# Two transformer blocks on one core: the branch for overfull experts moves behind the expert pass, and four handovers between stages are ordered anew

## The chip, the core and the metric

The kernel runs on one core of a Trainium2 chip. The core has a matrix engine (TensorE, in the profile PE, its weight loads PEld), three other compute engines (VectorE or DVE, ScalarE or ACT, GpSimd or POOL) and a queue engine (SyncE or SP) that issues most of the transfers from memory. Each engine takes its own instructions in order; semaphores tie them together. The metric is the device time of one execution in microseconds (us), as the median of several runs.

## The reference

The input is one sequence of 256 tokens of width 1024, in fp32. Two blocks follow each other.

The first block has two layers. Each layer is a mixer (four kinds of attention, each on a quarter of the width) and a feed-forward part, both behind an RMS norm whose gain, shift and output gate come from a conditioning vector:

```python
x = x + g_m * (concat(o_a, o_b, o_c, o_d) @ w_out[l])
hn = adaln(x, ffn_norm_g[l], sh_f, sc_f)
f = swiglu(hn, ...) if l % 2 == 0 else moe_swiglu(hn, router, w1, w3, w2)
x = x + g_f * f
```

The feed-forward part of layer 0 is dense (width 2816). That of layer 1 is a mixture of 8 experts (width 3584): a router picks two experts for each token, and the output is the sum of their SwiGLU outputs, weighted by the softmax of the two logits. The first block ends in an RMS norm.

The second block is a dense FFN, an attention mixer (8 heads of neighbourhood attention, 8 heads of dilated attention, 64 wide) and another dense FFN, each with a norm before and after it:

```python
h = swiglu_2(rmsnorm_2(x, pre_g), w_gate, w_up, w_down)
x = x + 0.5 * rmsnorm_2(h, post_g)
```

## The kernel before, in words

The 256 tokens are two tiles of 128 (`t` = 0 and 1), held as `x[t]` with tokens on the partitions. A matrix product needs its left side with the width on the partitions, so each stage first transposes `x[t]` on PE and writes `hT[t]`.

**Products in three passes.** To keep fp32 accuracy, each operand is split into a rounded part `hi` and a rest `lo`, and `mm3` (lines 213 to 217) does three matmuls: hi by hi, hi by lo, lo by hi. Weights come in granules of at most 1 MB, 128 partitions by 2048 columns (`wload`, line 143, on SP's queue, into `st` or `sx` tiles). `wsplit` (line 173) makes `hi` on ACT (line 181) and `lo` on DVE (line 185), in pieces of at most `wide["step"]` columns, into a few rotating pairs of tiles. In the mixers of the first block that step is 1024 columns, elsewhere 2048. So every weight passes through SP, ACT, DVE and PE, in this order.

**Order.** A scheduler orders the instructions of each engine ahead of time, by the order of the program text and a model of their durations; so weights of a later stage can be loaded and split before an earlier stage is done, as far as tiles are free. `behind(ins, first)` (line 208) forces one instruction behind another in this order, without a wait. After a norm of tile 0 (`norm_ev`, line 284, or `scaled_hT`, line 303), `hold` notes its last two instructions on ACT and DVE; the weight pieces from column 2048 to column 5120, counted from there, are put behind them (lines 186 to 192). Tile 1 has no such rule. A run-time `tc.If` is one unit for the scheduler: nothing from outside is put inside.

**Expert pass.** Each expert takes its tokens into 128 slots. `moe()` (line 1325) routes, gathers the rows of expert 0, loads a register on every engine with the largest number of tokens that any expert has (line 1414), and branches (line 1415): if it is over 128, a second pass with other slot numbers (`moe_pass` with `rnd` = 1) adds what the first 128 slots leave out. Behind this stands the common pass (`rnd` = 0): 8 experts by 7 blocks of 512 columns. For each block PE does up and gate products into two PSUM banks (`eh`), then the down products of the block before (`down`, line 1135, into two banks `eo`, one per half of the width). The outputs of experts 0 to 6 are written to DRAM and gathered back by token; they are added to `x` by `moe_combine` (line 1080), for tile 0 and tile 1 at blocks 5 and 6 of the last expert. Those of expert 7 are put back by `scatter` (line 1104) after its last product: for each half, split, two matmuls per token tile with a 0/1 matrix (`ohT`), two DVE sums per tile into `x`.

**Behind the pass.** Lines 1649 to 1658 transpose and scale `x[t]` whole, sum its squares, take the reciprocal roots, and multiply `x`; `dense_ffn` (line 454) then runs with weights g1, g3, g2. In its block 0 (256 columns) it does tile 0's gate and value products over the whole depth of 1024, then tile 1's.

**Mixer of the second block.** `mix2` (line 1440) projects q, k and v, and for each of four groups of heads transposes q into `qT` and k into a block-diagonal `kb`, zeroed by POOL before: two heads lie on partitions 0 to 63 and 64 to 127, each with 256 columns of its own, so that one matmul of 128 rows by 512 columns (line 1478) gives the logits of two heads:

```python
p = aps("lg2")
nc.tensor.matmul(p.rearrange("p (a b) -> p a b", a=2), qT[:, hp, t * T:(t + 1) * T],
                 kb[:, hp, :, :], start=True, stop=True)
```

Of the kernel before, what the change touches and what calls it, by code (L numbers as in the profile page):

```python
# [11 lines left out]
I32 = mybir.dt.int32  # L12
# [29 lines left out]
HELD_FROM = 2048  # L42
HELD = 3072
# [52 lines left out]
def kernel(ctx: ExitStack, tc: tile.TileContext, a: dict, out: bass.AP):  # L96
# [76 lines left out]
    def wsplit(ld, pool=None, pre="", late=False, after=None, into=None, at=0):  # L173
# [3 lines left out]
        step = max(n for n in (1, 2, 4) if n * w <= wide["step"])  # L177
        for k in range(0, nk, step):
# [27 lines left out]
    hold = {"ops": None, "skip": 0}  # L206
# [77 lines left out]
    def norm_ev(t, y, ps, hT, gain, shift=None):  # L284
# [15 lines left out]
        if t == 0:  # L300
            hold.update(ops=ops, skip=HELD_FROM)

    def scaled_hT(t, hT, gain):
# [10 lines left out]
        if t == 0:  # L314
            hold.update(ops=ops, skip=HELD_FROM)
# [138 lines left out]
    def dense_ffn(hT, w1, w3, w2, post, hook=None, r=None):  # L454
        with ExitStack() as es:
# [5 lines left out]
            acc = [[aps(f"fo{t}{n}") for n in range(2)] for t in range(2)]  # L461
# [13 lines left out]
            for b in range(nb + 1):  # L475
                gT = [None, None]
                if b < nb:
# [22 lines left out]
                    if b == 0:  # L500
# [69 lines left out]
    def transpose_p(ap, pt, lg, idx, nk):  # L570
        nkc = nk // T
        per_bank = 4 // nkc
        for i0 in range(0, len(idx), per_bank):
            sub = idx[i0:i0 + per_bank]
            p = hps("ptr")
            for j, i in enumerate(sub):
                for kc in range(nkc):
# [3 lines left out]
                 p[:, :len(sub) * nk].rearrange("p (a b c) -> p a b c", a=len(sub), b=nkc))  # L581

# [402 lines left out]
    def moe_turn(mp, rnd, ps, oh, tp=None, xg=None):  # L985
# [6 lines left out]
        def step(i):  # L992
# [20 lines left out]
            ohT = (tp or mp).tile([T, 256], F32R, tag="ohT", name="ohT", bufs=2)  # L1013
# [12 lines left out]
    def moe_slots(pool, posm, yd):  # L1026
        sel, gate = rt["sel"], rt["gate"]
        zero = small([T, 9], I32, name="zslot", bufs=1)
        nc.vector.memset(zero, 0)
        tab = dram.tile([T * 9, 1], I32, name="slots")  # L1030
# [4 lines left out]
        for t in range(2):  # L1035
            ok = small([T, 8], name="pok")
            nc.vector.scalar_tensor_tensor(ok, posm[t], 128.0, sel[t], op0=ALU.is_le, op1=ALU.mult)
            v = small([T, 8], name="pv")
            nc.vector.scalar_tensor_tensor(v, posm[t], 8.0, erow, op0=ALU.mult, op1=ALU.add)
            nc.vector.tensor_tensor(v, v, ok, op=ALU.mult)  # L1040
# [9 lines left out]
            none = small([T, 2], name="pnone")  # L1050
            nc.vector.tensor_scalar(none, ab, 0.0, 1025.0, op0=ALU.is_equal, op1=ALU.mult)
            put = small([T, 2], I32, name="pput")
            nc.vector.scalar_tensor_tensor(put, ab, -1.0, none, op0=ALU.add, op1=ALU.add)
            for i in range(2):
                nc.gpsimd.indirect_dma_start(tab[:, :], bass.IndirectOffsetOnAxis(ap=put[:, i:i + 1], axis=0),
                                             tok[:, t:t + 1], None)
            nc.vector.tensor_tensor(ok, ok, enot, op=ALU.mult)
# [40 lines left out]
    def moe_pass(mp, gp, rnd, gate, posm, yh, yl, grow, ld_fn, split_fn, first=None, yd=None):  # L1098
# [43 lines left out]

        nxt = first or gather(0)
        prev = None
        done = None
        for e in range(NE):
            xh, xl, ohT = nxt
            acc = [aps(f"eo{n}") for n in range(2)]
            for b in range(nb):
# [7 lines left out]
                for wi, nm in enumerate(("e1", "e3")):  # L1157
# [9 lines left out]
                    if wi == 0:  # L1167
                        nc.scalar.activation(s, p, AF.Silu)
                    else:
                        nc.vector.tensor_tensor(g, s, p, op=ALU.mult)  # L1170
                if prev is not None:
                    down(prev[1], prev[2], prev[3], gT)
                if done is not None and b == 1:
                    if rnd:
                        scatter(*done)
                    else:
                        keep(done[0], done[1])
                    done = None
                if b == 0 and e > 0:
                    done = (e - 1, prev[1], prev[4])  # L1180
# [9 lines left out]
                if b == nb - 3 and e + 1 < NE:  # L1190
# [4 lines left out]
                    turn = moe_turn(gp, rnd, None, oh, None, xg)  # L1195
# [4 lines left out]
                if e == NE - 1 and b >= 5:  # L1200
# [124 lines left out]
    def moe():  # L1325
        sel, gate = rt["sel"], rt["gate"]
        with tc.tile_pool(name="mo", bufs=1, reuse_waits="tile") as mo, \
# [34 lines left out]
            with tc.manual_schedule():  # L1362
# [37 lines left out]
                nc.vector.tensor_copy(mxi, mx)  # L1400
                trn = moe_turn(mo, 0, gp, oh)
# [12 lines left out]
            most = nc.values_load(mxi[0:1, 0:1], min_val=0, max_val=256)  # L1414
            with tc.If(most > T):  # L1415
                with tc.tile_pool(name="mq", bufs=1) as mq:
                    moe_pass(mq, mo, 1, gate, posm, yh, yl, grow,
# [377 lines left out]
```

## Time and profile before

| | us |
|---|---|
| median of 3 runs | 2085.16 (2085.03 to 2085.52) |
| profiled execution | 2086.3 |
| its span, first to last instruction | 2084.5 |
| PE busy in the span | 2015.6 |
| DVE busy | 1590.2 |
| ACT busy | 1251.4 |

The mean granted clock of PE is 0.983 of full speed. In rows of time order, an `x4` behind a row means four instructions of a kind in a row, and the bracket gives the engine's idle time before it and what ended it. A matmul's own duration is longer than the distance to the next, because matmuls overlap; the distance between two starts is what it costs. The engine names with a q (PEq, ACTq) are the engines' sequencers.

### The profile page before, as it was taken

The numbers are of one execution on the slowest core, as the hardware profiler recorded it, in microseconds if no ns is written. First come the engines' busy times: TensorE is split into PE (matmuls) and PEld (weight loads), VectorE is DVE, ScalarE is ACT, GpSimd is POOL, SyncE is SP. The second block draws the span as 40 slices with busy tenths as digits, with TensorE's granted clock in tenths as the row PEclk, the third lists the DMA queues.
The fourth block names the chain that finished last, engine by engine and source line by source line (L and its number), as shares of the span: only waits on it lengthen the run. The fifth ranks groups of instructions, "written<-read, shape, count | busy, mean of one in ns | idle before, by whom it ended". The sixth has DMA issues, their size and how long they took to land.

```text
span 2084.5 us, 24737 instructions
## 1 busy us (share of the span) xinstructions
PE 2015.6 (97%) x9369; PEld 1623.0 (78%) x9370; DVE 1590.2 (76%) x2044; ACT 1251.4 (60%) x1469; POOL 37.1 (2%) x37
## 2 busy tenths in 40 slices
PE   7999999999899999999999999999989999998998
PEld 3867888777678888888888888888768886777886
DVE  6897878797688888888888888888895446556544
ACT  3766434476377777777777777777654345655442
POOL 0000000000000000000000000001000000000000
PEclk9999999999899999999999999999999999999999
DMA  8846876484499999999999999999966534436530
GB/s 331 292 177 256 353 292 242 173 233 150 154 340 379 366 369 374 385 380 382 379 386 379 378 378 378 383 363 399 396 243 240 185 101 163 165 135 228 202 122 20
DMA packets 89809, 586.38 MB, mean 281 GB/s; under 512 B 12880, under 2 KB 13776, under 8 KB 23376
## 3 DMA queue, kind: packets, MB, share of 16 engines
q1 hardware_dynamic: 81184, 566.05, 72.2%
q10 hardware_dynamic: 6432, 11.84, 1.6%
q0 software_dynamic: 2064, 6.83, 0.9%
q8 instruction: 75, 1.23, 0.2%
q14 instruction: 54, 0.44, 0.1%
HBM read 578.89 MB, written 5.78 MB: 280 GB/s over the span
## 4 chain that ended last, share of the span: by engine, by line
PE 67%; DVE 3%; ACT 1%; issue 1%; DVEq 0%; ACTq 0%
PE eh L215 10%; PE eh L216 10%; PE eh L214 10%; PE eo L215 5%; PE eo L216 5%; PE eo L214 5%; PE ff L214 4%; PE ff L215 4%; PE ff L216 4%; PE fo L214 2%; PE fo L215 2%; PE fo L216 2%; DVE lo L185 1%; PE egt L1129 1%; PE pj L216 1%
## 5 line engine op out<-in xcount | busy, mean ns | idle before, releaser
L185 DVE TENSOR_TENSOR lo<-st,hi 128x2048 fp32r<-128x2048 f32 (+2 forms) x327 | 648.1, 2002 | 138.2 <-ACT hi L181 131.2
L181 ACT CAST hi<-st 128x2048 fp32r<-128x2048 f32 (+2 forms) x328 | 540.2, 1681 | 156.9 <-PE ff L216 58.7
L185 DVE TENSOR_TENSOR lo<-sx,hi 128x2048 fp32r<-128x2048 f32 (+1 forms) x200 | 451.8, 2274 | 131.5 <-ACT hi L181 128.8
L181 ACT CAST hi<-sx 128x2048 fp32r<-128x2048 f32 (+1 forms) x200 | 374.5, 1899 | 136.5 <-PE ff L216 97.0
L214 PE MATMUL eh<-hi,xeh 128*128 128x512 f32 x896 | 351.4, 392 | 8.2 <-PEq L1415 5.1
L215 PE MATMUL eh<-lo,xeh 128*128 128x512 f32 x896 | 353.3, 394 | 2.4 <-DVE lo L185 2.4
L216 PE MATMUL eh<-hi,xel 128*128 128x512 f32 x896 | 350.4, 391 | 0.0
L214 PE MATMUL ff<-hi,hTh 128*128 128x512 f32 (+1 forms) x576 | 221.6, 385 | 10.5 <-DVE hTl L312 4.6
L215 PE MATMUL ff<-lo,hTh 128*128 128x512 f32 (+1 forms) x576 | 217.1, 377 | 1.5 <-DVE lo L185 1.5
L216 PE MATMUL ff<-hi,hTl 128*128 128x512 f32 (+1 forms) x576 | 217.4, 378 | 0.1
L214 PEld LDWEIGHTS eh<-hi,xeh 128*128 128x128 f32 x896 | 169.1, 189 | 45.2 <-ACTq L1415 5.5
L215 PEld LDWEIGHTS eh<-lo,xeh 128*128 128x128 f32 x896 | 169.2, 189 | 41.3 <-DVE lo L185 7.1
L216 PEld LDWEIGHTS eh<-hi,xel 128*128 128x128 f32 x896 | 169.2, 189 | 34.5
L215 PE MATMUL eo<-lo,egh 128*128 128x512 f32 x448 | 179.7, 401 | 0.3 <-DVE lo L185 0.3
L214 PE MATMUL eo<-hi,egh 128*128 128x512 f32 x448 | 175.2, 391 | 0.7 <-ACT egh L220 0.7
L216 PE MATMUL eo<-hi,egl 128*128 128x512 f32 x448 | 174.9, 390 | 0.5 <-DVE egl L220 0.5
L214 PEld LDWEIGHTS ff<-hi,hTh 128*128 128x128 f32 x576 | 111.5, 194 | 29.9 <-DVE hTl L312 4.8
L214 PE MATMUL pj<-hi,hTh 128*128 128x512 f32 (+3 forms) x320 | 123.9, 388 | 4.2 <-ACT hTh L220 3.1
L215 PEld LDWEIGHTS ff<-lo,hTh 128*128 128x128 f32 x576 | 111.5, 194 | 20.0 <-DVE lo L185 2.0
L216 PEld LDWEIGHTS ff<-hi,hTl 128*128 128x128 f32 x576 | 111.2, 193 | 20.1 <-DVE hTl L220 0.4
L216 PE MATMUL pj<-hi,hTl 128*128 128x512 f32 (+3 forms) x320 | 122.7, 384 | 3.4 <-DVE hTl L220 1.9
L215 PE MATMUL pj<-lo,hTh 128*128 128x512 f32 (+3 forms) x320 | 125.1, 391 | 0.9 <-DVE lo L185 0.8
(383 smaller groups left out, 2611.3 us busy)
## 6 DMA issues: line engine op xcount, KB each, us to landing
st<-in_e_dram SPq DMA_DIRECT2D x192, 1024.0 KB, 7.4
sx<-in_e_dram SPq DMA_DIRECT2D x144, 1024.0 KB, 7.6
st<-in_ada_dram SPq DMA_DIRECT2D x30, 1024.0 KB, 5.1
sx<-in_g_dram SPq DMA_DIRECT2D x19, 1024.0 KB, 6.0
sx<-in_h_dram SPq DMA_DIRECT2D x19, 1024.0 KB, 4.9
sx<-in_ada_dram SPq DMA_DIRECT2D x18, 1024.0 KB, 10.3
st<-in_w_in_dram SPq DMA_DIRECT2D x16, 1024.0 KB, 5.0
sx<-in_f_dram SPq DMA_DIRECT2D x15, 1024.0 KB, 7.0
```

Source lines behind the costliest of these rows:

```text
L181: c = nc.scalar.copy(hi[:, d], st[:, s])
L185: d = nc.vector.tensor_tensor(*rest.pop(), op=ALU.subtract)
L214: m = nc.tensor.matmul(ps, xh, wh, start=start, stop=False)
L215: nc.tensor.matmul(ps, xh, wl, start=False, stop=False)
L216: nc.tensor.matmul(ps, xl, wh, start=False, stop=stop)
L1129: nc.tensor.transpose(p[:, j * T:(j + 1) * T], g[:, j * T:(j + 1) * T], ident)
```

## The change

1. **The branch.** The `tc.If` with the second pass stands behind the common pass. Its register loads come in the middle of that pass, at the first block of expert 6. For this, expert 7's `ohT` gets a tile that lives on, and the slot table covers 16 times 128 entries, so tokens beyond the 128 slots have a place in it (three small DVE operations fewer).
2. **The end of the pass.** For the last expert, `finish_last` does the last two blocks' down products half by half: both for half 0, then half 1, with the scatter of half 0 (`back(0)`) in between. The scatter of half 1 is returned as `rest` and called later. The two combines come at blocks 4 and 5.
3. **The start of the next FFN.** `dense_ffn` takes a function `start`. Its block 0 then runs over half the depth for both tiles and both weights, into four PSUM banks, then over the other half. `start(0)` transposes and scales half 0 of both tiles, calls `rest()`, and sums squares; `start(1)` does half 1; `start(2)` takes the roots. The norm's two sums come from `x` and from `x` times its gain, for both tiles at once.
4. **Holds.** Weight pieces from column 2048 to 5120 are put behind tile 0's last instructions, and those from 4096 to 8192 behind tile 1's. Pieces are at most 1024 columns up to column 4096 after tile 0's norm, and throughout `mix2`.
5. **Logits of the second block.** k is kept as it is, one copy per tile and no zeroing; each head's logits are a matmul of 64 rows by 256 columns, the two heads of a pair into two banks.

```diff
-HELD_FROM = 2048
-HELD = 3072
+HELD = ((2048, 5120), (4096, 8192))
+FINE = 4096
@@ wsplit
-        step = max(n for n in (1, 2, 4) if n * w <= wide["step"])
+        step = max(n for n in (1, 2, 4) if n * w <= (1024 if hold["n"] < FINE else wide["step"]))
...
-            if hold["ops"] is not None:
-                if hold["skip"] <= 0:
-                    behind(c, hold["ops"][0])
-                    behind(d, hold["ops"][1])
-                hold["skip"] -= min(step, nk) * w
-                if hold["skip"] < -HELD:
-                    hold["ops"] = None
+            for first, last, ops in hold["ops"]:
+                if first <= hold["n"] < last:
+                    behind(c, ops[0])
+                    behind(d, ops[1])
+            hold["n"] += min(step, nk) * w
@@ norm_ev, scaled_hT
-        if t == 0:
-            hold.update(ops=ops, skip=HELD_FROM)
+        holds(t, ops)
@@ dense_ffn
+                    if b == 0 and start is not None:
+                        lds = {(wi, kg): wload("f1", flat, kg) for kg in range(2) for wi, flat in enumerate((w1, w3))}
+                        p = {(t, wi): aps(f"ff{wi}{t}") for t in range(2) for wi in range(2)}
+                        for kg in range(2):
+                            start(kg)
+                            hl = pair()
+                            ws = [wsplit(lds[wi, kg], into=hl, at=wi * 4 * w) for wi in range(2)]
+                            for t in range(2):
+                                for wi in range(2):
+                                    up(p[t, wi], t, kg, ws[wi])
+                        start(2)
...
@@ moe_pass
+        def finish_last(acc, ohT, gT, g):
...
+            def back(n):
+                sl = slice(n * 512, n * 512 + 512)
+                e = wk.tile([T, D], F32R, tag="y", name="eys", bufs=2)
+                split_to(halves(e)[0], halves(e)[1], acc[n])
+                for t in range(2):
+                    p = (pps if n else hps)("sct")
+                    for i in range(2):
+                        nc.tensor.matmul(p, ohT[:, t * T:(t + 1) * T], halves(e)[i], start=i == 0, stop=i == 1)
+                    nc.vector.scalar_tensor_tensor(p, p, gate[t][:, NE - 1:NE], grow[:, sl], op0=ALU.mult, op1=ALU.mult)
+                    nc.vector.tensor_tensor(x[t][:, sl], p, x[t][:, sl], op=ALU.add)
+
+            products(0, nb - 2, gT)
+            g = transposes(g)
+            products(0, nb - 1, g)
+            products(1, nb - 2, gT)
+            back(0)
+            products(1, nb - 1, g)
+            return lambda: back(1)
...
+                if rnd == 0 and e == NE - 1 and b == nb - 1:
+                    return finish_last(acc, ohT, gT, g)
...
+                if e == NE - 2 and b == 0:
+                    rt["most"] = nc.values_load(rt["mxi"][0:1, 0:1], min_val=0, max_val=256)
...
-                if e == NE - 1 and b >= 5:
+                if e == NE - 1 and b >= 4:
                     behind(add.pop(0)(), m)
@@ moe
-            most = nc.values_load(mxi[0:1, 0:1], min_val=0, max_val=256)
-            with tc.If(most > T):
-                ...
             with tc.tile_pool(name="mp", bufs=2, reuse_waits="tile") as mp:
...
+            with tc.If(rt["most"] > T):
+                with tc.tile_pool(name="mq", bufs=1) as mq:
+                    moe_pass(mq, mo, 1, gate, posm, yh, yl, grow,
...
+        return rest
@@ mix2
-            widen(ap, MIX_PAIRS[1])
+            widen(ap, MIX_PAIRS[1], 1024)
...
+                for k in range(4):
+                    hp, i = divmod(k, 2)
+                    r = slice(i * 64, (i + 1) * 64)
+                    nc.tensor.matmul(p[i][:, hp * nk:(hp + 1) * nk], qT[r, hp, t * T:(t + 1) * T],
+                                     kT[r, hp, :nk], start=True, stop=True)
...
-                kb = ap.tile([T, 2, 2, 256], F32, tag="k2", name="k2", bufs=2)
-                nc.gpsimd.memset(kb, 0.0)
+                kb = ap.tile([T, 2, 256], F32, tag="k2", name="k2", bufs=2)
...
@@ behind the pass
+    def start1(h):
+        if h < 2:
+            for t in range(2):
+                scaled_half(t, h, hT, fgain)
+            if h == 0:
+                rest()
...
```

## Rows read from the trace of the kernel before

**Rows 1.** The page: busy time; groups with busy time, mean ns, idle before.

```profile
PE 2015.6 (97%) x9369; PEld 1623.0 (78%) x9370; DVE 1590.2 (76%) x2044; ACT 1251.4 (60%) x1469; POOL 37.1 (2%) x37
...
L185 DVE TENSOR_TENSOR lo<-sx,hi 128x2048 fp32r<-128x2048 f32 (+1 forms) x200 | 451.8, 2274 | 131.5 <-ACT hi L181 128.8
...
L181 ACT CAST hi<-sx 128x2048 fp32r<-128x2048 f32 (+1 forms) x200 | 374.5, 1899 | 136.5 <-PE ff L216 97.0
```

**Rows 2.** Stretches: length, busy times by engine, PE clock, DMA share, GB/s.

```profile
564.00:583.00 19.00, 10.59 (x27) 7.16 (x26) 10.80 (x22) 10.61 (x8) 5.17 (x5) 0.62 0.32 99
1500.00:1520.00 20.00, 17.57 (x77) 13.71 (x76) 19.09 (x13) 11.68 (x9) 0.00 (x0) 1.00 0.77 269
1520.00:1563.00 43.00, 34.11 (x177) 27.95 (x176) 39.42 (x80) 24.23 (x46) 0.00 (x0) 0.88 0.68 255
1737.00:1757.00 20.00, 15.81 (x63) 11.15 (x61) 17.30 (x50) 15.61 (x30) 0.00 (x0) 0.91 0.62 223
1760.00:1870.00 110.00, 109.10 (x560) 84.57 (x559) 57.87 (x141) 65.80 (x145) 1.90 (x2) 1.00 0.43 147
1880.00:1900.00 20.00, 14.27 (x86) 12.86 (x86) 16.23 (x48) 14.80 (x31) 0.00 (x0) 0.83 0.63 247
```

**Rows 3.** Line 1415, the branch: ns min/median/max, first and last start.

```profile
L1415 PEldq COMPARE_BRANCH  x1: 5872/5872/5872, 563.3 to 563.3; - x1
L1415 ACTq COMPARE_BRANCH  x1: 50/50/50, 564.9 to 564.9; - x1
L1415 DVEq COMPARE_BRANCH  x1: 72/72/72, 565.1 to 565.1; - x1
L1415 DVEq EVENT_SEMAPHORE  x1: 21/21/21, 568.9 to 568.9; - x1
```

**Rows 4.** PE in order of time at the start of the expert pass.

```profile
563.64 0.64 PE L1012 MATMUL ohT<-gen,oh 128*128 128x128 f32 x2
...
569.37 0.76 PE L214 MATMUL eh<-hi,xeh 128*128 128x512 f32 x1 [5.10 <-PEq L1415]
...
574.20 0.63 PE L216 MATMUL eh<-hi,xel 128*128 128x512 f32 x1
...
576.63 0.49 PE L214 MATMUL eh<-hi,xeh 128*128 128x512 f32 x1 [1.80 <-ACT hi L181]
...
582.26 0.40 PE L216 MATMUL eh<-hi,xel 128*128 128x512 f32 x1
```

**Rows 5.** PE in order of time at the end of the expert pass.

```profile
1519.85 0.39 PE L214 MATMUL eo<-hi,egh 128*128 128x512 f32 x1
...
1522.57 0.39 PE L214 MATMUL eo<-hi,egh 128*128 128x512 f32 x1
...
1541.16 1.97 PE L307 MATMUL trx<-gen,x 128*128 128x128 f32 x8 [1.68 <-DVE x L1116]
...
1542.78 0.56 PE L214 MATMUL ff<-hi,hTh 128*128 128x256 f32 x1
...
1562.31 0.40 PE L215 MATMUL ff<-lo,hTh 128*128 128x512 f32 x1
```

**Rows 6.** DVE in order of time, the scatter's sums of one half.

```profile
1535.01 1.42 DVE L1114 SCALAR_TENSOR_TENSOR sct<-sct,gate,row 128x512 f32<-128x512 f32 x2 [0.59 <-PE sct L1113]
...
1536.33 1.28 DVE L1116 TENSOR_TENSOR x<-sct,x 128x512 f32<-128x512 f32 x2
```

**Rows 7.** The page: DMA issues, KB each, median us from issue to landing.

```profile
sx<-in_g_dram SPq DMA_DIRECT2D x19, 1024.0 KB, 6.0
```

**Rows 8.** PE in order of time, logits of the second block's attention.

```profile
1771.06 3.67 PE L1478 MATMUL lg<-k,q 128*128 128x512 f32 x8 [0.32 <-ACT k L566]
```

**Rows 9.** DVE in order of time, into the last FFN.

```profile
1887.49 2.29 DVE L185 TENSOR_TENSOR lo<-sx,hi 128x2048 fp32r<-128x2048 f32 x1
```

**Rows 10.** PE in order of time: into the projections, into the last FFN.

```profile
1751.61 0.50 PE L216 MATMUL pj<-hi,hTl 128*128 128x512 f32 x1 [1.59 <-DVE hTl L312]
...
1893.59 0.58 PE L214 MATMUL ff<-hi,hTh 128*128 128x256 f32 x1 [4.60 <-DVE hTl L312]
```

More of the change, by code (lines that the diff above doesn't have):

```diff
@@ L204, in wsplit, with holds @@
         return finish
-    hold = {"ops": None, "skip": 0}
+    hold = {"ops": [], "n": 0}
+    def holds(t, ops):
+        if t == 0:
+            hold.update(ops=[], n=0)
+        hold["ops"].append((*HELD[t], ops))
     def behind(ins, first):
@@ L299, in norm_ev, with scaled_half @@
             ops = split_to(hT[t][0][:, c:c + 4, :], hT[t][1][:, c:c + 4, :], full)
-        if t == 0:
-            hold.update(ops=ops, skip=HELD_FROM)
+        holds(t, ops)
+    def scaled_half(t, h, hT, gain):
+        p = hps("trx")
+        for j in range(4):
+            nc.tensor.transpose(p[:, j * T:(j + 1) * T], halves(x[t])[h][:, j * T:(j + 1) * T], ident)
+        for j in range(4):
+            c, src = 4 * h + j, p[:, j * T:(j + 1) * T]
+            g = gain[:, c:c + 1]
+            nc.scalar.activation(hT[t][0][:, c, :], src, AF.Copy, scale=g)
+            nc.vector.scalar_tensor_tensor(hT[t][1][:, c, :], src, g, hT[t][0][:, c, :].bitcast(F32),
+                                           op0=ALU.mult, op1=ALU.subtract)
     def scaled_hT(t, hT, gain):
@@ L460, in dense_ffn @@
             es.callback(stages, None)
-            acc = [[aps(f"fo{t}{n}") for n in range(2)] for t in range(2)]
+            if start is None:
+                acc = [[aps(f"fo{t}{n}") for n in range(2)] for t in range(2)]
             nb = len(FF_BLOCKS)
@@ L581, in transpose_p, with row_logits, f @@
                  p[:, :len(sub) * nk].rearrange("p (a b c) -> p a b c", a=len(sub), b=nkc))
+    def row_logits(bank, t, nk, qT, kT):
+        p = []
+        def f(h):
+            if not p:
+                p.extend(bank(f"lgr{i}") for i in range(2))
+                for k in range(4):
[3 more added lines that the diff above has]
+                                     kT[r, hp, :nk], start=True, stop=True)
+            hp, i = divmod(h, 2)
+            return p[i][:, hp * nk:(hp + 1) * nk]
+        return f
     def pv(po, pt, heads, v, nk):
@@ L1012, in step @@
                 nc.tensor.transpose(q[:, t * T:(t + 1) * T], oh[t].bitcast(F32), ident)
-            ohT = (tp or mp).tile([T, 256], F32R, tag="ohT", name="ohT", bufs=2)
+            ohT = sml.tile([T, 256], F32R, name="ohL") if keep else (tp or mp).tile([T, 256], F32R, tag="ohT", name="ohT",
+                                                                                    bufs=2)
             nc.scalar.copy(ohT, q[:, :256])
@@ L1141, in down, with products @@
                         b == 0 and k == 0, b == nb - 1 and k == 3)
+        def finish_last(acc, ohT, gT, g):
+            def products(n, b, g):
+                ws = split_fn(ld_fn("e2", "e2", 2 * b + n, NE - 1))
+                for k in range(4):
+                    mm3(acc[n], g[0][:, k * T:(k + 1) * T], g[1][:, k * T:(k + 1) * T], *ws[k],
+                        False, b == nb - 1 and k == 3)
+            def back(n):
[15 more added lines that the diff above has]
+            return lambda: back(1)
         nxt = first or gather(0)
@@ L1147, in moe_pass @@
             xh, xl, ohT = nxt
-            acc = [aps(f"eo{n}") for n in range(2)]
+            if not rnd or e == 0:
+                acc = [aps(f"eo{n}") for n in range(2)]
             for b in range(nb):
@@ L1173, in moe_pass @@
                 if done is not None and b == 1:
[L1174 to L1177, printed above, removed]
+                    keep(*done)
                     done = None
                 if b == 0 and e > 0:
-                    done = (e - 1, prev[1], prev[4])
+                    if rnd:
+                        scatter(e - 1, prev[1], prev[4])
+                    else:
+                        done = (e - 1, prev[1])
                 prev = (g, acc, e, b, ohT)
@@ L1542, in mix2 @@
                     nc.scalar.activation(qT[:, :, t * T:(t + 1) * T], p4[:, 0:2, :], AF.Copy, scale=0.125)
-                    for g in range(2):
-                        evac(kb[g * 64:(g + 1) * 64, :, g, t * T:(t + 1) * T], p4[g * 64:(g + 1) * 64, 2:4, :])
+                    evac(kb[:, :, t * T:(t + 1) * T], p4[:, 2:4, :])
                 for t in range(2):
```

87 lines of the change are left out of this document (47 added, 40 removed).

## The prediction

> **What bounds the kernel now.** The page's busy line comes first: TensorE (PE) is at work 97% of the span, so a saving counts only where PE is seen idle, or slow, or doing work that can go [rows 1]. The stretch table says where that is: in the expert pass and in the down and up projections PE is full, and the losses sit in four short places, where one stage hands over to the next. From 564 to 583 us PE works 10.59 of 19 us at a mean granted clock of 0.62; from 1520 to 1563 us 34.11 of 43 at 0.88; from 1737 to 1757 us 15.81 of 20 at 0.91; from 1880 to 1900 us 14.27 of 20 at 0.83. The attention of the second block, 1760 to 1870 us, is full: 109.10 of 110 [rows 2]. The lines of the branch, L1415 [rows 3], and PE's order of time [rows 4, 5] then say who ends each wait. One full-rate matmul of 512 columns takes (1522.57 - 1519.85)/12 = 0.227 us, at half clock (574.20 - 569.37)/11 = 0.44 us; the 256-column ones I take at half of that.
>
> **The branch leaves the start of the pass (A).** PE ends the last transposes at 564.28 (563.64 + 0.64) and starts the first expert matmul at 569.37, after 5.10 us for PEq L1415 [rows 4]. PE's compare-and-branch takes 5872 ns where ACT's takes 50, and DVE, whose branch is at 565.1, signals only at 568.9, 3.8 us later [rows 3]. PE then does 12 matmuls at half clock, waits 1.80 us more for the next hi part, and is at full rate from 582.26, when 21 matmuls are done [rows 4]. Without the branch PE goes on at 564.3. The next hi and lo, 1.90 and 2.27 us [rows 1], can be there at 564.9 + 4.2 = 569.1, counted from where ACT's branch stood [rows 3]; at half clock the first 12 matmuls last to 569.5, so this hides them. Twelve at 0.44, nine at 0.227 and 1 us for a wait give 564.3 + 5.3 + 2.0 + 1.0 = 572.6 where 582.26 stood: 9.7 us. I take 9, for the slot work of DVE that now competes with the lo parts. Bounds: 5.1 (the wait alone) and 13 (21 at full rate). The five register loads move into the pass, where PE has matmuls queued: nothing.
>
> **The end of the pass (B).** From the first matmul of the last down products, 1519.85, to the first 512-column matmul of the next FFN, 1562.31, are 42.5 us [rows 5]. The work in them at full rate is 48 down matmuls (10.9), 8 scatter matmuls (1.8), 96 of 256 columns (10.9) and some 20 transposes (2.2, by the 256-column price): 25.8 us. So 16.7 us are waits and half clock: the scatter of both halves stands behind the last product, DVE does 1.42 + 1.28 us of it per half [rows 6], and only then come the transposes, 1.68 us late [rows 5]. After: the first half is scattered while PE does the second half's products, the second while PE does the FFN's first half. What is added is the branch. It stands behind the last 12 products, which PE holds for 2.7 us, so of its 5.87 us 3.2 show [rows 3]; DVE's 3.8 run beside that. Then 1.6 us from the transposes to the first matmul (1541.16 to 1542.78 [rows 5]), 2.6 us for half clock (the 0.88 over 43 us [rows 2]), 0.7 for the last block's turn, 1.7 for weight parts that were cut ahead of time and now may stand behind the branch; and the second combine comes one block earlier, where the first left PE 2.43 us idle (20 - 17.57 [rows 2]). Sum 25.8 + 3.2 + 1.6 + 2.6 + 0.7 + 1.7 + 2.4 = 38.0: a gain of 4.5 us. Upper bound, branch covered and combine absorbed: 25.8 + 1.6 + 2.4, a gain of 12.7. Lower bound: all 5.87 show, and a weight load (6.0 us to landing [rows 7]) and one hi and lo (1.90, 2.27 [rows 1]) stand open behind it in place of the 1.7: 49.2, a loss of 6.7.
>
> **Logits of the second block (C).** Four groups, two token tiles and two head pairs make 16 calls; a call leaves two records, eight of them take 3.67 us [rows 8], 0.46 each: 14.7 us of a stretch where PE is full. After, 32 calls of half the rows and half the columns make 64 records of 0.23 us: the same 14.7 if they run one after the other. No row shows two matmuls side by side. Two neighbours sit in different halves of the rows and write different banks, but each call's own two records share one half, so at best only every second pair can overlap: eight records of a unit in five steps, 0.69 us saved per unit, 5.5 over eight units. I take off 0.25 per unit as an estimate for switching and get 3.5. Bounds: -2 (no overlap, switching paid) and 7.3 (half). [...] The zeroing of the key tile on POOL and half of ACT's key copies go too; neither is on the path.
>
> **The second token tile before the weights (D, E).** Into the last FFN, DVE puts lo parts of 2.29 us between the second tile's hTl, and PE waits 4.60 us for them at 1893.59 [rows 9, 10], then runs at half clock: 0.83 over 20 us is 6.8 us at half, 3.4 lost [rows 2], of which I count 2.6 after this wait. After, weights from column 4096 on are put behind the tile. Next late is the second block's first weight: 1.90 + 2.27 us after the tile, while PE has 48 matmuls of 0.114, 5.5 us; ACT's sums of squares may go in between. I give back 2.7 of the 7.2 and take 4.5 (bounds 0, 7.2). Into the second block's projections the wait is 1.59 us [rows 10] with 0.09 x 20 = 1.8 us of clock [rows 2]; of 3.4 I take 2 (bounds -1, 3.4). The two handovers inside the first block wait for the first tile's chain, which the change leaves: 0, within 1 either way. Cutting weights in 1024 columns adds a start-up to each piece on ACT and DVE, which are busy 65.80 and 57.87 of 110 us where it is done throughout [rows 2]: nothing.
>
> **Sum.** 9 + 4.5 + 3.5 + 4.5 + 2 = 23.5 us. The profiled execution took 2086.3 us (span 2084.5); the median of the runs, 2085.16, is 1.1 lower. 2086.3 - 23.5 - 1.1 = 2061.7: 2062 us.
>
> **Rivals.** (1) *The branch is only moved*: with its full 5.87 us and the next weights behind it, B is -6.7 and the sum 12.3: 2073 us. For it: L1415 stalls each engine after its own branch [rows 3], and DVE's last sums and the transposes hang on each other across it. Against: PE has 12 products in hand, and SP runs far ahead. [...]
> (2) *The held weights starve PE* (slower): behind each second tile the next weight's hi and lo, 4.2 us, stand open because PE has used up the first block's matmuls, and the clock halves, 2.6 more: 6.8 us at each of five handovers, 34 us, and D and E are gone: 9 + 4.5 + 3.5 - 34 = -17, 2102 us. It decides where a block's 96 matmuls of 0.114 (10.9 us) end before the tile and 4.2 us are over. Against: at 1893 us the tile would end some 4 us earlier than now, with 5.5 us of matmuls left.
> (3) *Everything at the end of the pass is covered*: B is 12.7, the sum 31.7: 2053 us. For it: only PE's branch is long, and PE's sequencer was ahead of its matmuls at 563.3 [rows 3, 4].
> (4) Rival 1 with the starving of rival 2 at the last FFN alone: 9 - 6.7 + 3.5 + 2 - 6.8 = 1.0, 2084 us: no change.
>
> **Numbers.** Forecast 0.63, rival 1 0.16, rival 3 0.10, rival 2 0.07, rival 4 0.04. Of a kernel like this some 0.2% can be told from no change, 4 us. Faster: 0.63 + 0.16 + 0.10 = 0.89; same 0.04; slower 0.07. The range reaches from below rival 3, 2049, to above rival 1, 2077; beyond it lie rivals 2 and 4 and the tails of A and C, some 0.2 together. The forecast's own range is 2055 to 2069.
>
> **What would show it.** A: no row of the branch near 564, the first expert matmul within 0.5 us of the last transposes, full rate before 575. B: PE's compare-and-branch now behind the last products, PE idle some 3 us there, no scatter wait of DVE before the transposes of the first half; 38 us between the same two matmuls. C: eight records of a unit in about 1.1 us, not 1.8. D: no wait for hTl over 1 us in the last FFN, and no half clock behind it. Wrong if PE waits over 8 us behind the branch, if a wait for hi or lo of the second weight block takes the place of the one for hTl, or if the logits keep their 14.7 us.

## The result and the profile after

The changed kernel takes 2058.47 us (median of 4 runs, 2056.25 to 2061.16), the kernel before, run beside it, 2085.34 (2085.03 to 2087.81): a ratio of 0.9869, 95% interval 0.9852 to 0.9886, or 24 to 31 us. The forecast was 2062, range 2049 to 2077. The profiled execution took 2056.25 us with a span of 2054.5; the mean granted clock is 0.992. It is the fastest of the four, and the other three show 0.988 to 0.991.

Where the time went is read from matmuls that stand in both programs: the distance between two of them is the time of a stage. First PE in order of time in the kernel before, then in the changed one: first row transpose of expert 0 and of expert 7, first down product of the next FFN, first projection and last output product of the second mixer, last down product.

```profile
560.02 1.12 PE L1001 MATMUL xtr<-gen,xg 128*128 128x128 f32 x4 [0.68 <-ACT xg L996]
...
1353.09 0.60 PE L1001 MATMUL xtr<-gen,xg 128*128 128x128 f32 x4
...
1584.62 0.39 PE L214 MATMUL fo<-hi,gh 128*128 128x512 f32 x1
...
1738.04 0.39 PE L214 MATMUL pj<-hi,hTh 128*128 128x512 f32 x1
...
1879.35 0.40 PE L216 MATMUL o<-hi,o2l 128*128 128x512 f32 x1
...
2076.36 0.39 PE L216 MATMUL fo<-hi,gl 128*128 128x512 f32 x1
```
```profile
557.99 1.12 PE L1044 MATMUL xtr<-gen,xg 128*128 128x128 f32 x4 [0.68 <-ACT xg L1039]
...
1338.82 0.60 PE L1044 MATMUL xtr<-gen,xg 128*128 128x128 f32 x4
...
1568.60 0.39 PE L217 MATMUL fo<-hi,gh 128*128 128x512 f32 x1
...
1722.04 0.39 PE L217 MATMUL pj<-hi,hTh 128*128 128x512 f32 x1
...
1855.01 0.40 PE L219 MATMUL o<-hi,o2l 128*128 128x512 f32 x1
...
2045.79 0.39 PE L219 MATMUL fo<-hi,gl 128*128 128x512 f32 x1
```

| stage | before | after | gain | forecast |
|---|---|---|---|---|
| up to the pass | 560.02 | 557.99 | 2.0 | 0 |
| start of the pass, up to expert 7 | 793.07 | 780.83 | 12.2 | A 9 |
| end of the pass, first FFN block | 231.53 | 229.78 | 1.8 | B 4.5 |
| rest of that FFN | 153.42 | 153.44 | 0 | 0 |
| second mixer | 141.31 | 132.97 | 8.3 | C + E 5.5 |
| last FFN | 197.01 | 190.78 | 6.2 | D 4.5 |

The stages add up to 30.6 us between these two executions; by the medians the gain is 26.9. Most stages repeat well from kernel to kernel (the last FFN took 190.76 to 190.82 us in ten of them). Two do not. The first took 557.5 to 563.4 us in 14 profiled executions, so its 2.0 us are no finding. The end of the pass took 228.41, 228.43, 228.52, 229.78 and 231.92 us in five programs that have the same text there (the changed kernel and four of the experiments below), so its 1.8 us are one value out of a range from a gain of 3.1 to a loss of 0.4. What differs is mostly the clock. Three windows show it (columns as in [rows 2]), all some 166 us behind the last expert's first row transpose: without the branch (no_branch), in the shortest of the five (same_half) and in the longest (rows_mix1).

```profile
1507.00:1565.00 58.00, 53.28 (x281) 45.03 (x280) 46.57 (x80) 33.77 (x55) 0.00 (x0) 0.97 0.75 295
```
```profile
1510.00:1568.00 58.00, 51.28 (x270) 43.32 (x269) 44.91 (x79) 32.90 (x55) 0.00 (x0) 0.97 0.74 294
```
```profile
1510.00:1568.00 58.00, 50.55 (x255) 42.76 (x254) 44.78 (x79) 31.66 (x54) 0.00 (x0) 0.91 0.75 292
```

The stretches that answer to [rows 2], moved by as much as the stage starts earlier (columns as there):

```profile
562.00:581.00 19.00, 18.84 (x85) 14.98 (x84) 18.96 (x29) 15.71 (x14) 5.67 (x3) 0.98 0.89 299
1506.00:1549.00 43.00, 38.65 (x215) 33.26 (x214) 35.26 (x58) 26.34 (x46) 0.00 (x0) 0.96 0.64 247
1721.00:1741.00 20.00, 18.46 (x85) 14.15 (x84) 17.02 (x52) 16.21 (x36) 0.00 (x0) 1.00 0.45 145
...
1856.00:1876.00 20.00, 18.58 (x119) 15.93 (x119) 17.03 (x50) 17.10 (x30) 0.00 (x0) 1.00 0.58 212
```

PE is now busy 18.84 of the first 19 us where it was 10.59, and its clock is 0.98 where it was 0.62; in the last stretch 18.58 at 1.00 for 14.27 at 0.83. PE at the start of the pass, which answers to [rows 4], has hardly a wait left (0.16 us from 560 to 570), and is at full rate 3 us after its first expert matmul, which now stands ahead of the second transposes:

```profile
559.82 0.75 PE L217 MATMUL eh<-hi,xeh 128*128 128x512 f32 x1
...
562.80 0.40 PE L218 MATMUL eh<-lo,xeh 128*128 128x512 f32 x1
...
563.50 0.60 PE L1044 MATMUL xtr<-gen,xg 128*128 128x128 f32 x4
```

The branch, now line 1505, is in the rows that answer to [rows 3]:

```profile
L1505 PEldq COMPARE_BRANCH  x1: 3851/3851/3851, 1519.7 to 1519.7; - x1
L1505 ACTq COMPARE_BRANCH  x1: 50/50/50, 1520.1 to 1520.1; - x1
...
L1505 DVEq COMPARE_BRANCH  x1: 72/72/72, 1522.6 to 1522.6; - x1
...
L1505 DVEq EVENT_SEMAPHORE  x1: 21/21/21, 1525.6 to 1525.6; - x1
```

And PE's longer waits about it, in order of time: the two combines, the branch, and the gates of the next FFN's first block.

```profile
1480.93 0.50 PE L218 MATMUL eh<-lo,xeh 128*128 128x512 f32 x1 [1.79 <-DVE lo L185]
...
1500.47 0.50 PE L218 MATMUL eh<-lo,xeh 128*128 128x512 f32 x1 [1.86 <-DVE lo L185]
...
1525.74 1.94 PE L308 MATMUL trx<-gen,x 128*128 128x128 f32 x8 [2.59 <-DVEq L1505]
...
1557.09 0.50 PE L217 MATMUL ff<-hi,hTh 128*128 128x512 f32 x1 [2.45 <-ACT s L496]
```

### The profile page after: what moved, and what is told of

Read it like the earlier page. It is cut to its first block, busy times and chain, and to the rows that moved or that the text cites. A ratio compares the mean times of both kernels' runs of the same rounds, so it can differ in the third digit from the quotient of the medians.

```text
span 2054.5 us, 24792 instructions
## 1 busy us (share of the span) xinstructions
PE 1999.7 (97%) x9402; PEld 1617.0 (79%) x9402; DVE 1589.0 (77%) x2049; ACT 1249.1 (61%) x1476; POOL 38.4 (2%) x33
## 5 line engine op out<-in xcount | busy, mean ns | idle before, releaser
L219 PE MATMUL ff<-hi,hTl 128*128 128x512 f32 (+1 forms) x576 | 212.3, 374 | 0.4 <-DVE hTl L223 0.4
```

The lines of the kernel that those rows point to most:

```text
L219: nc.tensor.matmul(ps, xl, wh, start=False, stop=stop)
```

## The experiments

"End stretch" is the third stage of the table. Each is an edit of the changed kernel, where nothing else is said.

**The branch back in front (branch_front).**

```diff
+            most = nc.values_load(mxi[0:1, 0:1], min_val=0, max_val=256)
+            with tc.If(most > T):
+                ...
             rt.pop("mm", None)
...
-            with tc.If(rt["most"] > T):
```

> The changed kernel with its branch, and the register loads, back in front of the common pass; all else is as changed. By the prediction's steps, sized by the two traces: the stretch from the first row transpose of expert 0 to the first transposes of its gated block goes back from 18.3 to 31.1 us (12.8 us lost, less the 0.6 that the changed kernel gave back by expert 1), and the end of the pass, from the first row transpose of the last expert to the first down product of the next FFN, now 229.8 us, gets shorter by what the branch costs there: 2.6 us of waiting, the half clock and late weights behind it, 4 us. Median 2058.5 + 12.2 - 4 = 2066.7. Rival, the branch is only moved and its price goes with it: the end gets shorter by as much as the start gets longer, 2058.5 +- 1.5.

Measured: 2069.35 us, ratio 0.9915 (0.9901 to 0.9929). From the first row transpose to the first transposes of the gated block (egt) it takes 31.36 us (18.29 in the changed kernel), the end stretch 225.92. The first theory holds; the rival is 10 us off. PE in order of time, with the branch in front and then in the changed kernel, whose first row transpose is at 557.99:

```profile
560.94 0.66 PE L1044 MATMUL xtr<-gen,xg 128*128 128x128 f32 x4 [0.68 <-ACT xg L1039]
...
569.62 0.76 PE L217 MATMUL eh<-hi,xeh 128*128 128x512 f32 x1 [4.96 <-PEq L1487]
...
592.30 0.60 PE L1171 MATMUL egt<-gen,eg 128*128 128x128 f32 x4
```
```profile
576.28 0.60 PE L1171 MATMUL egt<-gen,eg 128*128 128x128 f32 x4
```

**No branch (no_branch).**

```diff
-                if e == NE - 2 and b == 0:
-                    rt["most"] = nc.values_load(rt["mxi"][0:1, 0:1], min_val=0, max_val=256)
...
-            with tc.If(rt["most"] > T):
-                ...
```

> The changed kernel without the branch and without its register loads: the second pass for overfull experts is left out. Prices the branch where it now stands. By the prediction (3.2 us shown, 1.7 for weight parts that stand behind it, some of 2.6 for the half clock): the stretch from the first row transpose of the last expert to the first down product of the next FFN falls from 229.8 to 224 or 225 us, median 2053. Rival (the branch runs beside what the end of the pass waits for anyway: the scatter's sums and the norm's roots): it falls by less than 1.5 us, median 2057 or more. Start of the pass as in the changed kernel, 18.3 us, in both.

Measured: 2056.94 us, ratio 0.9857 (0.9842 to 0.9872); end stretch 225.90, as with the branch in front. Against the changed kernel's profiled execution the branch costs 3.9 us. But that one ran at half clock once more, behind the second combine (0.72 from 1500 to 1506 us, where same_half shows 1.00 from 1505 to 1511): three experiments below with the same end show 228.41, 228.43 and 228.52, by which the branch costs 2.5. A fourth, rows_mix1, shows 231.92, by which it costs 6.0; there the clock behind the branch is 0.91 over 58 us, for the 0.97 of same_half and of this run. So 2.5 us is the price at the same clock; whether the branch makes the longer half clock more frequent, these executions don't show. The prices of 2.5 and 3.9 lie between the two expectations. Without it the transposes follow the last product at once:

```profile
1522.89 0.39 PE L219 MATMUL eo<-hi,egl 128*128 128x512 f32 x1
1523.12 1.03 PE L308 MATMUL trx<-gen,x 128*128 128x128 f32 x8
```

**The old end, branch behind it (old_end).** The start of the next FFN is the text of before.

```diff
-                if rnd == 0 and e == NE - 1 and b == nb - 1:
-                    return finish_last(acc, ohT, gT, g)
...
-                if e == NE - 1 and b >= 4:
+                if e == NE - 1 and b >= 5:
...
-    dense_ffn(hT, ..., r=r1, start=start1)
+    dense_ffn(hT, ..., r=r1)
```

> The changed kernel with the end of the pass and the start of the next FFN as before (scatter of both halves behind the last product, combines at blocks 5 and 6, tile 0's products over the whole depth first), and the branch behind it all. By the prediction the twelve products that PE has in hand cover 2.7 us of the branch and the order by halves covers the scatter: without them the stretch from the first row transpose of the last expert to the first down product of the next FFN is the 231.5 us of before and the whole of PE's branch, 5.9 us: 237.4, median 2058.5 + 7.6 = 2066. Rival, the new order is worth only what it saved with the branch away (231.5 - 225.9 = 5.6) and the branch costs its 3.9 anywhere: 235.4, median 2064. A third, DVE's sums and the split of the scatter cover the branch as well as the products do: 231.5, median 2060.

Measured: 2064.64 us, ratio 0.9897 (0.9882 to 0.9912); end stretch 233.85. The branch costs 2.3 us here (231.53 before, without it), 2.5 behind the new order. That the two agree is in part chance: the kernel before differs from this one in its holds and pieces too, PE waits 5.18 us before the transposes here for 1.68 there, later waits are shorter, and the clock differs (0.88 over the 58 us from 1505 here, 0.91 over those from 1520 there). What the rows do show is that the twelve products in hand buy nothing: without them, too, DVE goes on last, behind PE's record.

```profile
L1503 PEldq COMPARE_BRANCH  x1: 3814/3814/3814, 1524.2 to 1524.2; - x1
...
L1503 DVEq COMPARE_BRANCH  x1: 72/72/72, 1526.2 to 1526.2; - x1
...
L1503 DVEq EVENT_SEMAPHORE  x1: 21/21/21, 1529.3 to 1529.3; - x1
```
```profile
1529.51 1.94 PE L320 MATMUL trx<-gen,x 128*128 128x128 f32 x8 [5.18 <-DVEq L1503]
```

The new order is worth 5.4 us with the branch behind it and 5.6 without. So the stretch comes nearest to the rival; its price of 3.9 was too high.

**Logits by 64 rows alone (rows_alone).** An edit of the kernel before.

```diff
-                    cache = {}
-                    ...
+                    lgf = row_logits(aps, t, 256, qT, kb)
...
-                kb = ap.tile([T, 2, 2, 256], F32, tag="k2", name="k2", bufs=2)
-                nc.gpsimd.memset(kb, 0.0)
+                kb = ap.tile([T, 2, 256], F32, tag="k2", name="k2", bufs=2)
```

> The kernel before with the logits by 64 rows alone. Prediction's C, sized by the trace: 1.56 us a unit fall to 0.96, eight units, 4.8 us; the stretch from the second mixer's first projection to its last output product goes from 141.3 to 136.5 us and the median from 2085.3 to 2080.5. Rival, that mixer's gain of 8.3 us came from the holds and the finer weight pieces, and what the logits save is waited out behind the softmax: 141 us, median 2085. A third, that the saved zeroing and copies let the first unit start sooner: 134 us, median 2078.

Measured: 2084.95 us, ratio 0.9988 (0.9979 to 0.9997); second mixer 138.68 us, 2.6 less. The logits themselves take 4.1 us less of PE (added up from each group's start to the next instruction), and PE's waits in the mixer grew from 4.8 to 6.6 us. None of the three numbers; the first, less new waits.

**Another order in a unit (same_half).**

```diff
-                    hp, i = divmod(k, 2)
+                    i, hp = divmod(k, 2)
                     r = slice(i * 64, (i + 1) * 64)
```

> The changed kernel with the four logit matmuls of a unit in another order: both of the first 64 rows, then both of the last 64, where the two halves alternated. By the prediction's picture two neighbouring records overlap only where they lie in different halves of the rows: eight records are five steps when the halves alternate (0.96 us measured, 5/8 of eight times 0.195) and seven steps in this order, 1.37 us. Eight units lose 0.41 us each: the stretch from the second mixer's first projection to its last output product grows from 133.0 to 136.2 us, median 2061.8. Rival, a matmul of 64 rows is cheaper by itself, whatever stands beside it: 0.96 us a unit, 133.0 us, no change.

Measured: 2059.61 us, ratio 0.9864 (0.9848 to 0.9879), not told apart from the changed kernel; second mixer 136.46 us. The stage's number came as forecast, and its reason is refuted: from the first start to the next instruction's, eight records take 1.07 us here and 1.06 in the changed kernel. What differs is PE's waits (3.6 us for 2.1) and the clock, 0.91 over 20 us where the changed kernel's stage has 1.00:

```profile
1770.00:1790.00 20.00, 19.52 (x107) 15.70 (x106) 12.07 (x36) 12.70 (x34) 0.00 (x0) 0.91 0.50 174
```

Narrow windows show why the order is nothing. PE in order of time, the first and the last two records of a unit, in the changed kernel and in this one: the last row of each holds two records in the 0.38 us that one takes. In both orders records start two at a time, from the second pair on 0.22 us apart. The rows don't name the half that a record lies in; that each pair is one of either half is inferred.

```profile
1767.85 0.49 PE L620 MATMUL lgr<-k,q 64*128 64x256 f32 x2
...
1768.60 0.38 PE L620 MATMUL lgr<-k,q 64*128 64x256 f32 x2
```
```profile
1772.16 0.49 PE L620 MATMUL lgr<-k,q 64*128 64x256 f32 x2
...
1772.92 0.39 PE L620 MATMUL lgr<-k,q 64*128 64x256 f32 x2
```

**256 columns of 128 rows (cols256).** An edit of the kernel before.

```diff
-                            nc.tensor.matmul(p.rearrange("p (a b) -> p a b", a=2), qT[:, hp, t * T:(t + 1) * T],
-                                             kb[:, hp, :, :], start=True, stop=True)
+                                nc.tensor.matmul(p2[j][:, hp * 256:(hp + 1) * 256], qT[:, hp, t * T:(t + 1) * T],
+                                                 kb[:, hp, j, :], start=True, stop=True)
```

> The kernel before with the logits of each head by a matmul of its own: all 128 rows of q, the zero-padded k, 256 columns instead of 512, in the order and the banks of the changed kernel. It asks what made the 64-row records cheap, 0.12 us each, where half of a 512-column one is 0.195. If it is the rows: a record of 256 columns takes 0.195 and eight of a unit 1.56 us as before, the second mixer stays at 141 us. If it is the columns (a matmul of 512 fp32 columns is slow by itself): 0.12 and 0.96 us, and the mixer falls to 138.7 as with the logits by 64 rows.

Measured: 2088.63 us, a single run; second mixer 141.42 us. It is the rows: these records start one at a time, eight take 1.80 us.

```profile
1793.44 0.67 PE L1479 MATMUL lgr<-k,q 128*128 128x256 f32 x2
1793.73 0.59 PE L1479 MATMUL lgr<-k,q 128*128 128x256 f32 x2
1793.95 0.59 PE L1479 MATMUL lgr<-k,q 128*128 128x256 f32 x2
```

(Three overlapping windows; each first start is the next record's, 0.22 to 0.29 us on.)

**No hold for tile 1 (no_hold1).**

```diff
-HELD = ((2048, 5120), (4096, 8192))
+HELD = ((2048, 5120), (0, 0))
```

> The changed kernel without the rule for the second token tile (the weight pieces from column 4096 to 8192 are no longer put behind it); the finer pieces stay. By the prediction's D and E, sized by the traces: the last FFN (from the last output product of the mixer to the last down product), 190.8 us, goes back to the 197.0 of before, and the second mixer, 133.0 us, towards the 138.7 that the logits alone leave: 6.2 + 5.7, median 2058.5 + 11.9 = 2070.4. Rival, the gain comes from the pieces of 1024 columns, which let a tile's small operations in between: both stretches stay within 1 us, median 2059.

Measured: 2069.64 us, ratio 0.9923 (0.9910 to 0.9937); second mixer 137.79 us, last FFN 195.82: 4.8 and 5.0 us lost. The first theory holds in the main, the rival is refuted. Its waits in the two stages, then the largest that the changed kernel has left for hTl:

```profile
1741.19 0.50 PE L217 MATMUL pj<-hi,hTh 128*128 128x512 f32 x1 [2.35 <-ACT n L1536]
...
1875.59 0.58 PE L217 MATMUL ff<-hi,hTh 128*128 128x256 f32 x1 [4.61 <-DVE hTl L325]
```
```profile
1865.12 0.39 PE L217 MATMUL ff<-hi,hTh 128*128 128x256 f32 x1 [0.26 <-DVE hTl L325]
```

**Coarse pieces (coarse).**

```diff
-FINE = 4096
+FINE = 0
...
-            widen(ap, MIX_PAIRS[1], 1024)
+            widen(ap, MIX_PAIRS[1])
```

> The changed kernel with weight pieces of 2048 columns again, behind each norm and in the second mixer; the holds of both tiles stay. Theory (the hold alone does it, as the prediction's D and E have it, with nothing for the pieces): 133.0 and 190.8 us stay within 1 us, median 2059. Rival (the pieces do it): 138 and 197 us, median 2070. A third, both are needed: a piece of 2048 columns that stands behind the tile comes whole 2 us later, and the first matmuls of the next block wait for it: some 2 us at each of the two, 2062.

Measured: 2060.42 us, ratio 0.9872 (0.9857 to 0.9887); last FFN 190.76, second mixer 135.26 us. In the last FFN the hold does it all; in the mixer the pieces are worth 2.3 us, as the third theory had it for both places.

**Towards a better version.** The first three are single runs, so their times prove little, and their stages are read. One_root:

```diff
-        root(s[4], s[5])
-        ...
-        root(s[9], s[10])
-        tt(s[10], s[10], s[5], op=ALU.mult)
+        nc.vector.scalar_tensor_tensor(s[4], s[0], D * EPS, s[1], op0=ALU.add, op1=ALU.add)
+        nc.vector.tensor_tensor(s[5], s[2], s[3], op=ALU.add)
+        nc.vector.scalar_tensor_tensor(s[5], s[4], EPS, s[5], op0=ALU.mult, op1=ALU.add)
+        rsqrt(v, y, u, z, r, math.sqrt(D))
```

> The changed kernel, with one reciprocal root in place of two at the start of the next FFN (the scale of the gates is written as a root of its own sum, so both roots go through one chain of small operations) and the scaling of x put behind the gates. It asks what the 2.45 us are that PE waits at the end of that FFN's first block for the gates. If it is the chain of the two roots with the scaling of x and the lo parts between (DVE, 1547.15 to 1555.20): the wait falls under 1 us, and the stretch from the first row transpose of the last expert to the first down product, 228.5 us in most executions, to 226.5. Rival, the lo parts of the next weights are what DVE is late with: PE then waits for lo instead, 228 us.

Measured (one_root): 2054.73 us; the wait of 2.45 is gone, end stretch 226.22. The first theory holds; the edit also puts the scaling of x behind the gates, and the two aren't told apart.

Spread (the other two pieces of a tile are the last two lines of `add`, one block later):

```diff
-            f = nc.vector.tensor_scalar(g[0], g[0], w[:, 0:1], None, op0=ALU.mult)
+            nc.scalar.activation(g[0], g[0], AF.Copy, scale=w[:, 0:1])
...
-                if e == NE - 1 and b >= 4:
-                    behind(add.pop(0)(), m)
+                if e == NE - 1 and b >= 3:
+                    for op in add.pop(0)():
+                        behind(op, m)
```

> The changed kernel with each combine cut in two, its first operation on ACT: half a combine in each of the last expert's blocks 3 to 6 in place of a whole one in blocks 4 and 5. If DVE's load of a block is what makes PE wait (0.39 + 1.79 us at the first combine, 0.15 + 1.86 at the second, all for lo): the four waits fall to 1 us together, the same stretch goes from 228.5 to 225. Rival, DVE is so full in this pass that any added work is waited out, wherever it stands, and the half beside the last down products delays the first scatter: 228 us or more.

Measured (spread): 2070.57 us, end stretch 243.69. Neither: the waits for lo fell to 2.2 us, but the operation that was moved to ACT was put in front of the arrival of its data and held up ACT, and so PE:

```profile
1424.34 1.15 ACT L1133 ACTIVATE ycomb<-ycomb,pw 128x1024 f32<-128x1024 f32 x1 [11.26 <-DMA ycomb<-eod,pget]
```

Rows_mix1 (k copied as it is, as in the second block):

```diff
-                return head_unit(t, 6, lambda: pair_logits(t, qTd, kbd), lambda lg: (lambda h: dba(t, h)),
+                return head_unit(t, 6, lambda: row_logits(aps, t, NK[t], qTd, kbd), lambda lg: (lambda h: dba(t, h)),
```

> The changed kernel with the logits by 64 rows also in the third and fourth attention of the first block's mixers, where k was zero-padded too. A unit of 256 keys saves 0.6 us as in the second block, one of 128 keys half of it; four of each: 3.6 us over the two mixers, 1.8 in each. From the first projection of the second mixer to the first row transpose of the pass 164.7 us now, 162.9 then; from the first projection of the first mixer to the first transposes behind it 152.6 now, 150.8 then. Rival, the shorter logits only make PE wait for the softmax, as where they were put alone into the kernel before (2.6 of 4.8 us were kept): 0.9 in each.

Measured (rows_mix1): 2062.68 us; 165.47 us in the one mixer, 154.54 in the other, no gain that stands out of their spread (164.7 to 166.5 and 152.2 to 155.4 in the other executions). The reason is in the rows: there most records of 256 columns stand in groups of two or four, and such a group takes some 0.63 us, two records as long as four. The logits of both mixers take 8.8 us of PE for 10.2 in the changed kernel (from each group's start to the next instruction's, without waits): 1.3 saved where 3.6 were expected.

Best, one_root with:

```diff
-                if e == NE - 1 and b >= 4:
-                    behind(add.pop(0)(), m)
+                if e == NE - 1 and b >= 3:
+                    for _ in range((3, 3, 2)[b - 3]):
+                        behind(add.pop(0)(), m)
```

> The changed kernel with the one root (2.2 us measured in its single look) and the combines spread over the last expert's blocks 3 to 5, two or three operations to a block, each put behind that block's up products, so that the first of them, on ACT, can't stand in front of the transfer that it waits for (it stopped ACT for 11.26 us where it was not held). If the load of DVE per block is what makes PE wait: 4.45 us of waits for lo fall to some 2 (2.2 in the run before, with 1.2 more for the last piece beside the last down products, which is now away), the stretch from the first row transpose of the last expert to the first down product goes to 224, median 2058.5 - 2.2 - 2.2 = 2054. Rival, DVE is full there and waits out all that is added: 226.2, median 2056.

Measured (best): 2054.26 us (2053.74 to 2056.86), ratio 0.9855 (0.9839 to 0.9872); end stretch 226.15. The rival holds: the spread combine waits 3.9 us in seven small pieces where one_root waits 4.2. All the gain is the one root's, 2.3 us in the trace; by ratios this version isn't told apart from the changed kernel.

## Why the prediction was right, and where it was not

**A, 9 forecast, 12.2 measured.** The mechanism is shown (branch_front takes 13.1 us longer at the start). Too small was the term for what PE does meanwhile: twelve matmuls at half clock behind the last transposes. The branch had been a wall for the order, too: without it the first matmuls stand ahead of the second half's transposes (559.82 against 563.50), only some seven run at half clock, and the lo parts are there in time. 0.6 us were given back inside the pass; that was not followed up.

**B, 4.5 forecast, 1.8 in this execution, 3.1 by three others, a loss of 0.4 by a fourth.** The branch was priced at 3.2 us and shows 2.6 of waiting, 2.5 in all at the same clock. But its owner is another: PE's compare-and-branch, 3851 ns, is covered but for 0.4 us; PE waits for DVE, which reaches the branch at 1522.6, behind the issue of the first half's sums, and goes on 3.0 us later. The cover by PE's products, on which the step leaned, buys nothing, as DVE goes on last with or without it (old_end). The 1.7 us for weight parts behind the branch did not show: no wait for hi or lo there is over 0.3 us. The second combine costs 2.0 us more, as forecast (2.4). What is missing from the sum is the wait for the gates, 2.45 us: before, a wait of that kind was among the 16.7 us which the step replaced, and the new order keeps it. One_root, which shortens the chain of the two roots and moves the scaling of x, gives 2.2 of it back. Without the branch the new order gave 5.6 us, where the step's other terms make 9.4 (42.5 - 25.8 - 1.6 - 2.6 - 0.7 - 2.4). The missing 3.8 us are about what PE waits there besides: 2.45 us for the gates, 1.20 and 0.62 for hTl (no_branch).

**C, 3.5 forecast; D, 4.5; E, 2.** Added up from each group's start to the next instruction's, the logits took 13.5 us of PE before (32 records) and 10.2 after (64): 3.3 saved. (The prediction's 14.7 us counted the last record's own run in.) The size is right, the picture wrong, so the size is luck: not every second pair overlaps but every pair, in any order (0.22 us a pair, where in cols256 one record of 128 rows takes 0.22), and a group takes some 0.2 to 0.4 us more than its pairs (1.06 us for eight records, 0.62 for two). The 0.25 us per unit that the prediction took off for switching was the author's estimate from no row, and no run shows such a term; in its place the rows show 0.2 more for a whole unit, and three units are cut in two, which makes them 0.62 + 1.06 us where a whole one takes 1.06. Why a group costs more than its pairs, no run shows.

The hold gives 5.0 us in the last FFN (D) and 4.8 in the second mixer (E). In the last FFN PE's waits, added up, fell from 5.95 to 1.61 us and the clock rose from 0.98 to 1.00; of the 2.7 us that D gave back for the next weight nothing showed. E was bounded by 3.4, the one wait for hTl and its clock; outside the count were a later wait that the hold saves too, 2.35 us for ACT's copy of the first projection (no_hold1), and the finer pieces, costed at nothing and worth 2.3 us there (coarse), though a piece of 1024 columns takes more than half of one of 2048 (before: 1.05 us for 1.91 on ACT, 1.22 for 2.29 on DVE). The last 1.2 us of the last FFN are clock: rows_alone and no_hold1 take 195.8 us with the same waits as the kernel before. Here are the 16 us about the wait of 4.6 us, in the kernel before and in rows_alone; why the clock differs is open.

```profile
1889.00:1905.00 16.00, 11.41 (x62) 10.88 (x63) 11.20 (x30) 10.40 (x18) 0.00 (x0) 0.79 0.58 229
```
```profile
1890.00:1906.00 16.00, 11.39 (x69) 10.51 (x68) 12.22 (x30) 10.66 (x18) 0.00 (x0) 0.89 0.62 243
```

**The rest.** The register loads show no wait of their own, as forecast, but stand right before the branch on PE, ACT and DVE (1519.1 to 1522.0 us), not in the middle of the pass. Rival 1 falls with branch_front, rivals 2 and 4 with the waits: no hi or lo of the second block is waited for over 0.5 us in the last FFN. Rival 3 would need the branch for nothing. That the total came within 4 us of the forecast is in part luck: in the two profiled executions A, D and C with E gave 7.7 us more than forecast and B 2.7 less, and the gain by medians is 3.7 below the sum of the stages.

## What to carry to other kernels

A run-time branch is dear where everybody is empty-handed: here 13 us at the start of a stage, 2.5 at its end at the same clock. Price it by the engine that goes on last behind it, which need not be the one with the longest record: at the start it was PE (its semaphore row at 569.3 us, DVE's at 568.9), at the end DVE (1525.6, PE's 1523.6). Hold weight preparation behind the second tile as well as behind the first, where PE still has matmuls of the first. And when a total agrees with a forecast, read the rows of its mechanism all the same: twice here (C, same_half) the number was right and the reason was not.

## What the runs showed of the hardware

Where fp32 matmuls use the upper and the lower 64 rows by turns, their records start in pairs, 0.22 us a pair for 256 columns (the changed kernel), also where four of one half are issued before the four of the other (same_half); with 128 rows each record takes 0.22 us (cols256). Two records in a group take as long as four (some 0.63 us, rows_mix1), six as long as eight (1.06, the changed kernel).

The branch, which isn't entered in these runs, shows on PE as a record of 5872 ns in the kernel before, 3851 in the changed kernel and 3814 in old_end. The records of ACT and DVE are 50 and 72 ns, but the next semaphore row of the branch's line starts later: 4.1 us behind ACT's branch and 3.8 behind DVE's before, 2.5 and 3.0 in the changed kernel, 3.1 on DVE in old_end. How much of that the branch itself takes on ACT and DVE, the rows don't say.
